# HGRN heads of a hybrid backbone layer: the attention inside a chunk on column strips of the array, block by block

## Chip, core and metric

The kernel runs on one core of a Trainium2 chip, as one program. The metric is its device time in microseconds (us); the median of three runs before the change is 1113.08 us. The engines are named as the profile names them: PE is the matrix engine, PEld its weight loads, DVE the vector engine, ACT the scalar engine, POOL the GpSimd engine, SP the engine that issues most DMAs. [...]

## What is computed

One layer of a backbone over 512 latent tokens and 256 context tokens, 1024 wide: an adaptive norm, one combined input projection, two token mixers side by side, up-projections with gates, an output projection, and a SwiGLU block. Mixer A is a gated delta rule with four heads; mixer B is HGRN2 with four heads of 128 keys and 128 values, run in both directions. The change is in mixer B:

```
def hgrn2_chunk_scan(q, k, v, log_f, s0, with_output):
    lg = jnp.cumsum(log_f, axis=3)                        # within a chunk
    ...
    pair = jnp.exp(jnp.where(incl[:, :, None], lg_c[:, :, :, None, :] - lg_c[:, :, None, :, :], -jnp.inf))
    att = jnp.einsum('bhik,bhjk,bhijk->bhij', q_c, k_c, pair)
    o = jnp.einsum('bhck,bhkv->bhcv', q_c * jnp.exp(lg_c), s) + jnp.einsum('bhij,bhjv->bhiv', att, v_c)
```

The decay between two tokens differs for each of the 128 key channels, so `att` is no plain product of two matrices.

## The kernel before

**Levels.** The kernel takes chunks of 128 tokens, so a head has four chunks `c` of latents. For each of them it builds `AT`, the transposed 128 x 128 attention of both directions in one. The diagonal comes first (called level 7), then seven levels with b = 1, 2, 4, ..., 64 (levels 0 to 6). At level b, two tokens belong together when they lie in the two halves of one block of 2b tokens; for such a pair the decay can be split at the middle of the block, so that one factor goes with the key and one with the query. `kq[:, 0, :]` holds the keys and `kq[:, 1, :]` the queries with these factors, all 512 tokens wide. The function `att(kq, lvl)` then multiplies for each chunk all 128 keys by all 128 queries into a bank `pA` of PSUM, in fp32, with four matmuls of 128 x 128 x 128 (L477). Of that product a level needs only the pairs of its blocks. A predicated copy on DVE with a mask of 0 and 1 (`lev`, 128 columns for each of the seven levels) lays them into `AT` (L482); level 7 is laid in first, whole, by a copy on ACT (L480). Between two levels, DVE and ACT move the running sums K and L to the next b and build the next `kq` (L500 to L505): two exponentials on ACT, and on DVE one product and two updates of 128 x 512.

**After the levels** come the projection of the values (`values`, L105 and L448), the transposed keys (`pk`, `pkb`, L535), the states (`pS`, L540 and L543; `h_S` on DVE, L546), the output `po` (L552 to L554), which reads `AT`, and the norm of the head (L416 to L427), whose root is taken on POOL (L421).

**The order.** The four HGRN heads (streams H0 to H3), the two pairs of delta-rule heads (G0, G2) and the gate projections (`pgate`, called F where they fill in) are emitted in turns by a hand-written plan. The streams reach the engines' lists through the framework's scheduler, which orders them by priority and by its own estimate of when each instruction could start. So an instruction that the scheduler takes to be longer or shorter also moves others. In the names, `h` is an HGRN head, `p` and `g` belong to the delta rule: `p_Z` and `p_o` are steps of a triangular inverse on DVE, `p_T` its result after two transposes (L691, L692), `p_pR`, `p_pY`, `p_pX` and `p_pRb`, `p_pYb` its matmuls on tiles of 32 x 32 and 64 x 64 of the array (L724 to L753), `p_s` its scan over chunks. `mwb` are weights of the modulation that POOL loads and DVE sums up into `acc`. H0 to H3 run between about 270 and 600 us; the rest of the time after that goes to the merge, the output projection and SwiGLU, which the change doesn't touch.

## Time and profile before

| | |
|---|---|
| median of three runs | 1113.08 us (1111.55 to 1113.27) |
| span of the profiled execution, first to last instruction | 1115.9 us |
| instructions in the profile | 15740 |
| HBM read and written | 110.51 MB and 10.49 MB |
| mean granted clock of PE | 0.980 |
| attention matmuls `h_pA`, busy | 33.0 us for the seven levels (224 records) |
| masked copies into `h_AT` on DVE | 20.5 us (28 copies) |

The profiled execution has no time besides its span, which is 2.8 us above the median; differences are therefore worked out within the profile and taken from the median. A matmul in fp32 has two records in the profile, each with its weight load, so 112 matmuls are 224 records. A record's duration runs from its start to the end of its results and overlaps with the next record; what a matmul costs PE is the distance from one start to the next. In the rows of groups, the columns are line, engine, operation, output and inputs, shape and count, then busy time and mean duration, then idle time before them and who ended it. In the rows by tile, three durations are given: least, median and greatest, in ns.

### The profile page before, as it was taken

To read this page: it belongs to the slowest core of one execution; us is meant where nothing else is said; L and a number is where in the kernel's file an instruction comes from. 1 tells how busy PE (TensorE), PEld (TensorE's weight loads), DVE (VectorE), ACT (ScalarE), POOL (GpSimd) and SP (SyncE) were. 2 spreads that over 40 slices of the span, in tenths; PEclk is the share of its full clock that TensorE was granted. 3 is DMA by queue.
4 is the path that set the end of the run, shared out by engine and by line. 5 is a ranking of instruction groups with operands and counts; after the bars stand their busy time and mean duration, and the time that the engine had idled before them with its cause. 6 is when DMAs were issued, how large, how long until landed. Compare 5 with 4: busy or idle time off the path is not lost.

```text
span 1115.9 us, 15740 instructions
## 1 busy us (share of the span) xinstructions
PE 1054.0 (94%) x6007; PEld 879.1 (79%) x6007; DVE 696.8 (62%) x1365; ACT 560.1 (50%) x1062; POOL 75.8 (7%) x132
## 2 busy tenths in 40 slices
PE   4999999979999999999988999899999999999996
PEld 3787788858897887799777887787888888888785
DVE  5896877679676868866796675586343433422424
ACT  3454568747886765887764743452222222221212
POOL 0010000220001022000201000010000000000000
PEclk9998999989999999999999999999999999999999
DMA  9943322222003213200637853455333332322222
GB/s 303 283 149 109 114 76 57 58 76 57 3 20 114 76 48 86 57 2 11 194 118 227 299 153 123 129 167 159 93 93 94 94 88 80 93 94 94 92 95 94
DMA packets 142720, 122.02 MB, mean 109 GB/s; under 512 B 5534, under 2 KB 118452, under 8 KB 142644
## 3 DMA queue, kind: packets, MB, share of 16 engines
q1 hardware_dynamic: 135907, 100.20, 30.1%
q0 software_dynamic: 4640, 17.30, 4.8%
q10 hardware_dynamic: 2096, 3.50, 1.0%
q8 instruction: 47, 0.77, 0.3%
q14 instruction: 30, 0.24, 0.1%
HBM read 110.51 MB, written 10.49 MB: 108 GB/s over the span
## 4 chain that ended last, share of the span: by engine, by line
PE 57%; DVE 10%; issue 5%; ACT 3%; POOL 2%; DMA 2%; POOLq 0%; ACTq 0%; DVEq 0%
PE pf L105 19%; PE pfo L105 10%; PE pgate L105 4%; PE pup L105 4%; PE pwo L105 3%; PE h_z L105 2%; DMA mwb<-in_mod_w_dram 2%; PE h_pA L477 2%; PE h_zv L105 1%; DVE lo L97 1%; PE p_s_pk L778 1%; PE p_s_pk L787 1%; DVE p_o L683 1%; PE p_s_pk L775 1%; DVE p_Z L685 1%
## 5 line engine op out<-in xcount | busy, mean ns | idle before, releaser
L95 ACT CAST hi<-raw 128x1024 fp32r<-128x1024 f32 (+1 forms) x137 | 135.7, 991 | 307.4 <-PE pf L105 131.2
L97 DVE TENSOR_TENSOR lo<-raw,hi 128x1024 fp32r<-128x1024 f32 (+1 forms) x137 | 157.9, 1152 | 177.5 <-ACT hi L95 176.9
L105 PE MATMUL pf<-hhi,lo 128*128 128x512 f32 (+1 forms) x368 | 142.9, 389 | 2.4 <-DVE lo L97 2.4
L105 PE MATMUL pf<-hlo,hi 128*128 128x512 f32 (+1 forms) x368 | 143.0, 390 | 0.7 <-DVE hlo L1030 0.7
L105 PE MATMUL pf<-hhi,hi 128*128 128x512 f32 (+1 forms) x368 | 142.4, 390 | 0.0
L105 PEld LDWEIGHTS pf<-hhi,lo 128*128 128x128 f32 x368 | 69.8, 190 | 18.5 <-DVE lo L97 3.3
L105 PEld LDWEIGHTS pf<-hlo,hi 128*128 128x128 f32 x368 | 69.7, 190 | 16.5 <-DVE hlo L1030 1.1
L105 PEld LDWEIGHTS pf<-hhi,hi 128*128 128x128 f32 x368 | 69.7, 190 | 15.1
L105 PE MATMUL pfo<-lo,uh 128*128 128x512 f32 x176 | 69.8, 396 | 0.1
L105 PE MATMUL pfo<-hi,ul 128*128 128x512 f32 x176 | 69.5, 395 | 0.0
L105 PE MATMUL pfo<-hi,uh 128*128 128x512 f32 x176 | 68.7, 395 | 0.0
L105 PE MATMUL pgate<-hhi,lo 128*128 128x512 f32 x144 | 60.6, 422 | 6.7 <-DVE lo L97 6.7
L105 PE MATMUL pgate<-hhi,hi 128*128 128x512 f32 x144 | 61.1, 424 | 1.8 <-ACT hi L95 1.8
L105 PE MATMUL pgate<-hlo,hi 128*128 128x512 f32 x144 | 59.8, 416 | 0.0
L1053 DVE TENSOR_TENSOR sg<-sg,pf 128x512 f32<-128x512 f32 x22 | 15.1, 688 | 53.2 <-PE pf L105 53.2
L821 DVE SCALAR_TENSOR_TENSOR acc<-mwb,sc,acc 128x256 f32<-128x256 f32 x72 | 34.3, 482 | 13.0 <-DMA mwb<-in_mod_w_dram 11.7
L261 DVE SCALAR_TENSOR_TENSOR macc<-mw,sc,macc 128x256 f32<-128x256 f32 x96 | 40.0, 479 | 0.0
L105 PEld LDWEIGHTS pfo<-lo,uh 128*128 128x128 f32 x176 | 33.1, 188 | 8.7 <-DVE lo L97 1.0
L105 PEld LDWEIGHTS pgate<-hhi,lo 128*128 128x128 f32 x144 | 28.5, 198 | 14.4 <-DVE lo L97 9.2
L105 PE MATMUL h_z<-hhi,hi 128*128 128x512 f32 x96 | 39.3, 410 | 0.3 <-ACT abT L365 0.3
L105 PE MATMUL h_z<-hlo,hi 128*128 128x512 f32 x96 | 39.4, 411 | 0.0
L105 PEld LDWEIGHTS pfo<-hi,uh 128*128 128x128 f32 x176 | 32.9, 188 | 8.2 <-ACT hi L95 0.6
(422 smaller groups left out, 2566.3 us busy)
## 6 DMA issues: line engine op xcount, KB each, us to landing
raw<-in_ffn_w_in_dram SPq DMA_DIRECT2D x44, 512.0 KB, 3.9
raw<-in_w_in_dram SPq DMA_DIRECT2D x37, 512.0 KB, 3.9
raw<-in_ffn_w_out_dram SPq DMA_DIRECT2D x22, 512.0 KB, 3.5
mwb<-in_mod_w_dram POOLq DMA_DIRECT2D x18, 512.0 KB, 4.9
mw<-in_mod_w_dram SPq DMA_DIRECT2D x16, 512.0 KB, 6.3
mwe<-in_mod_w_dram POOLq DMA_DIRECT2D x7, 1024.0 KB, 6.2
gdram<-gt SPq DMA_DIRECT2D x24, 256.0 KB, 2.4
raw<-in_w_in_dram SPq DMA_DIRECT2D x18, 256.0 KB, 3.0
```

The costliest lines, as they stand in the source:

```text
L95: nc.scalar.copy(hi[:, :, :], raw[:, :, :])
L97: nc.vector.tensor_tensor(lo[:, :, :], raw[:, :, :], hi.bitcast(F32), op=ALU.subtract)
L105: nc.tensor.matmul(ps, a[u](k), b[v](k), start=(start and n == 0), stop=(stop and n == tot - 1))
L261: nc.vector.scalar_tensor_tensor(acc[:, :], mws[d][:, k, :], col, acc[:, :], op0=ALU.mult, op1=ALU.add)
L477: nc.tensor.matmul(pA[:, P * c:P * c + P], kq[:, 0, P * c:P * c + P], kq[:, 1, P * c:P * c + P], start=True, stop=True)
L683: nc.vector.tensor_tensor(ov, Z[:, r + 1:32, r:r + 1].to_broadcast([P, 31 - r, r]), Z[:, r:r + 1, 0:r].to_broadcast([P, 31 - r, r]), op=AL ...
L685: nc.vector.tensor_tensor(Z[:, r + 1:32, 0:r], Z[:, r + 1:32, 0:r], ov, op=ALU.add)
L775: nc.tensor.matmul(pk[:, 0:P], KTt[:, g, :], S[t][:, :], start=True, stop=True)
L778: nc.tensor.matmul(pk[:, P:2 * P], N[:, d, e, g, :], rt[:, :], start=True, stop=True)
L787: nc.tensor.matmul(pk[:, 2 * P:3 * P], kend[:, :], u[:, :], start=True, stop=True)
L821: nc.vector.scalar_tensor_tensor(acc[:, :], mw[:, k - k0, :], sc[:, k:k + 1], acc[:, :], op0=ALU.mult, op1=ALU.add)
L1053: nc.vector.tensor_tensor(sg[:, :], sg[:, :], pgu[1][:, :], op=ALU.mult)
```

## The change

The product of a level is computed only where the level keeps something. For the levels 0 to 4 and the diagonal (level 7), everything kept lies in the 32 x 32 blocks on the diagonal: a matmul takes 32 keys as weights on a strip of 32 columns of the array (all 128 rows, the key channels) and 32 queries, so each chunk has four matmuls, one on each strip. They write a new small tile `AD` (128 x 4 x 32) through a mask of 32 columns. Level 5 multiplies each block of 32 keys by its neighbour's queries, and level 6 each block of 64 keys by the other 64 queries, on strips of 64 columns. Nothing of levels 5 and 6 needs a mask: they are copied into `AT` by ACT, one copy for each strip (4 and 2). After level 4, POOL copies the four blocks of `AD` into `AT`. The mask's load shrinks from 896 to 160 columns.

```
-    lev = [(r // (2 * b) == c // (2 * b)) & (r // b != c // b) for b in LEVELS]
+    r, c = r % NB, c[:, 0:NB]
+    lev = [(r // (2 * b) == c // (2 * b)) & (r // b != c // b) for b in LEVELS[0:NSM]]
...
             AT = hg.tile([P, 4, P], F32, name=n + "AT", tag="AT")
+            AD = hg.tile([P, 4, NB], F32, name=n + "AD", tag="AD")
             def att(kq, lvl):
+                w = 64 if lvl == 6 else NB
                 pA = bank("ha", f"{n}pA{lvl}")
                 for c in range(4):
-                    nc.tensor.matmul(pA[:, P * c:P * c + P], kq[:, 0, P * c:P * c + P], kq[:, 1, P * c:P * c + P],
-                                     start=True, stop=True)
+                    for j in range(P // w):
+                        kt0, qt0 = P * c + w * j, P * c + w * (j ^ (lvl in (5, 6)))
+                        nc.tensor.matmul(pA[w * j:w * j + w, w * c:w * c + w], kq[:, 0, kt0:kt0 + w], kq[:, 1, qt0:qt0 + w],
+                                         start=True, stop=True, tile_position=(0, w * j))
+                pAv = pA[:, 0:4 * w].rearrange("p (c i) -> p c i", i=w)
                 if lvl == 7:
-                    nc.scalar.copy(AT[:, :, :], pA.rearrange("p (c i) -> p c i", i=P))
+                    nc.scalar.copy(AD[:, :, :], pAv)
+                elif lvl < NSM:
+                    nc.vector.copy_predicated(AD[:, :, :], lev[:, NB * lvl:NB * lvl + NB].unsqueeze(1).to_broadcast([P, 4, NB]), pAv)
                 else:
-                    nc.vector.copy_predicated(AT[:, :, :], lev[:, P * lvl:P * lvl + P].unsqueeze(1).to_broadcast([P, 4, P]),
-                                              pA.rearrange("p (c i) -> p c i", i=P))
+                    for j in range(P // w):
+                        s = slice(w * j, w * j + w)
+                        nc.scalar.copy(AT[s, :, w * (j ^ 1):w * (j ^ 1) + w], pAv[s, :, :])
+                if lvl == NSM - 1:
+                    for j in range(P // NB):
+                        s = slice(NB * j, NB * j + NB)
+                        nc.gpsimd.tensor_copy(AT[s, :, s], AD[s, :, :])
```

NB is 32 and NSM is 5. A head has 32 matmuls of attention before and 120 after (7 x 16 and 8). The other lines of the diff only drop comments, so line numbers after the first lines differ: L477 becomes L486, L482 becomes L492, L691 becomes L708.

The scheduler makes another order of the rest, from H0's attention on. Counted along PE's whole list, neighbouring matmuls differ in the shape of the array that they use (128 x 128; 32 x 32; 64 x 64; 128 rows by strips of 32 or of 64) 32 times before and 86 times after.

PE at the start of H0's attention; `g3_k_zl` is a projection of the delta rule. Before:

```order
L105 MATMUL g3_k_zl_3569<-hhi_73,lo35_3564 128x512
L477 MATMUL h0_pA7_3184<-h0_kqd_3178 128x128 x4
L477 MATMUL h0_pA0_3195<-h0_kq0_3190 128x128 x4
L105 MATMUL g3_k_zl_3569<-hhi_73,hi35_3562 128x512
L105 MATMUL g3_k_zl_3569<-hlo_74,hi35_3562 128x512
```

The same place now:

```order
L108 MATMUL g3_k_zl_3666<-hhi_73,lo35_3661 128x512
L486 MATMUL h0_pA7_3185<-h0_kqd_3179 32x32 x16
L486 MATMUL h0_pA0_3208<-h0_kq0_3203 32x32 x16
L108 MATMUL g3_k_zl_3666<-hhi_73,hi35_3659 128x512
L108 MATMUL g3_k_zl_3666<-hlo_74,hi35_3659 128x512
L108 MATMUL g3_k_zl_3666<-hhi_73,lo35_3661 128x512
L486 MATMUL h0_pA1_3233<-h0_kq1_3228 32x32 x16
L108 MATMUL g3_k_zl_3666<-hhi_73,hi35_3659 128x512
L108 MATMUL pgate2_2455<-hhi_73,lo20_2460 128x512
```

Sixteen matmuls on strips stand where four whole ones stood, level 1 (`pA1`) comes earlier among the projections, and a gate (`pgate2`) is drawn between them.

DVE at the end of the second triangular inverse (`p2_Z`, `p2_o`), with the first levels of H3 around it. Before:

```order
L685 TENSOR_TENSOR p2_Z_4221<-p2_Z_4221,p2_o29_4348 128x2x29
L502 TENSOR_TENSOR h3_kq1_5151<-h3_q_4949,h3_E1_5152 128x512
L683 TENSOR_TENSOR p2_o30_4351<-p2_Z_4221 128x30
L685 TENSOR_TENSOR p2_Z_4221<-p2_Z_4221,p2_o30_4351 128x30
L482 COPY_PREDICATED h3_AT_5125<-lev_864,h3_pA0_5143 128x512
L691 STREAM_TRANSPOSE p2_T1_4355<-p2_Z_4221 128x32x32
L692 STREAM_TRANSPOSE p2_T2_4356<-p2_Z_4221 128x32x32
L482 COPY_PREDICATED h3_AT_5125<-lev_864,h3_pA1_5156 128x512
```

The same place now:

```order
L519 TENSOR_TENSOR h3_kq4_5445<-h3_q_5143,h3_E4_5446 128x512
L702 TENSOR_TENSOR p2_Z_4415<-p2_Z_4415,p2_o29_4542 128x2x29
L522 TENSOR_TENSOR h3_L_5142<-h3_L_5142 128x2x16x16
L700 TENSOR_TENSOR p2_o30_4545<-p2_Z_4415 128x30
L492 COPY_PREDICATED h3_AD_5320<-lev_864,h3_pA4_5450 128x128
L702 TENSOR_TENSOR p2_Z_4415<-p2_Z_4415,p2_o30_4545 128x30
L521 TENSOR_TENSOR h3_K_5141<-h3_K_5141,h3_L_5142 128x2x8x32
L708 STREAM_TRANSPOSE p2_T1_4549<-p2_Z_4415 128x32x32
L709 STREAM_TRANSPOSE p2_T2_4550<-p2_Z_4415 128x32x32
```

Before, the transposes stood behind H3's level 0; now they stand behind its level 4, among the steps of the inverse.

POOL around H2's attention; `mwb` are loads of modulation weights, `h2_ss` belongs to the norm of the head. Before:

```order
L819 DMA mwb400_5534<-in_mod_w_dram 128x4x256
L819 DMA mwb404_5540<-in_mod_w_dram 128x4x256
L819 DMA mwb410_5548<-in_mod_w_dram 128x4x256
L819 DMA mwb414_5554<-in_mod_w_dram 128x4x256
L819 DMA mwb420_5596<-in_mod_w_dram 128x4x256
L819 DMA mwb424_5602<-in_mod_w_dram 128x4x256
L819 DMA mwb430_5610<-in_mod_w_dram 128x4x256
L421 TENSOR_TENSOR h2_ss_6140<-h2_ss_6140,mhalf_102 128x4
```

The same place now:

```order
L836 DMA mwb400_5825<-in_mod_w_dram 128x4x256
L836 DMA mwb404_5831<-in_mod_w_dram 128x4x256
L500 COPY h2_AT_6190<-h2_AD_6191 32x4x32 x4
L836 DMA mwb410_5839<-in_mod_w_dram 128x4x256
L836 DMA mwb414_5845<-in_mod_w_dram 128x4x256
L836 DMA mwb420_5887<-in_mod_w_dram 128x4x256
L836 DMA mwb424_5893<-in_mod_w_dram 128x4x256
L424 TENSOR_TENSOR h2_ss_6528<-h2_ss_6528,mhalf_102 128x4
```

The four copies stand in the middle of the weight loads, and the root of the norm one load earlier.

More of the change, by code (lines that the diff above doesn't have):

```diff
@@ L26 @@
 LEVELS = (1, 2, 4, 8, 16, 32, 64)
+NB = 32
+NSM = 5
 PADN = 8 * 68 + 260
@@ L331, in body @@
             columns(1)
[L332 to L333 removed]
+            lev = cp.tile([P, NSM * NB], U8, name="lev")
+            levf = s1.tile([P, NSM * NB], F32, name="levf")
             nc.sync.dma_start(levf[:, :], T["lev"])
```

2 lines of the change are left out of this document (removed).

## The prediction

> **What bounds the kernel now.** The page first: the busy share of each engine, then the slices.
>
> ```profile
> PE 1054.0 (94%) x6007; PEld 879.1 (79%) x6007; DVE 696.8 (62%) x1365; ACT 560.1 (50%) x1062; POOL 75.8 (7%) x132
> PE   4999999979999999999988999899999999999996
> ```
>
> PE is busy nearly everywhere, so a change pays where it shortens PE's own list or removes a wait of PE. Because a share is an average, the second view is the table by stretch over the 330 us in which the HGRN heads run.
>
> ```profile
> core 0: us, PE busy (x) PEld busy (x) DVE busy (x) ACT busy (x) POOL busy (x), PEclk, DMA share, GB/s
> 270.00:300.00 30.00, 28.43 (x433) 25.06 (x432) 22.93 (x42) 25.32 (x59) 0.90 (x2) 1.00 0.14 37
> 300.00:340.00 40.00, 40.00 (x322) 36.88 (x320) 30.20 (x73) 34.91 (x101) 1.01 (x1) 1.00 0.07 21
> ...
> 450.00:500.00 50.00, 48.23 (x561) 42.34 (x560) 36.62 (x70) 40.66 (x91) 0.91 (x2) 0.97 0.12 33
> ...
> 540.00:600.00 60.00, 52.99 (x309) 45.54 (x308) 50.32 (x99) 36.64 (x70) 9.03 (x12) 0.97 0.51 155
> sum 330.00, PE 312.54 PEld 273.33 DVE 250.31 ACT 237.29 POOL 36.98; mean PE 39.07 PEld 34.17 DVE 31.29 ACT 29.66 POOL 4.62
> ```
>
> PE idles 330.0 - 312.5 = 17.5 us of it. DVE is near its limit only in the last stretch, ACT in the second. The third view is what PE waits for there.
>
> ```profile
> PE pgate L105 <- DVE lo L97: 3.1, 3, 1.5
> PE h__pt L426 <- ACT h_on L423: 3.0, 3, 2.1
> PE p_pR L724 <- DVE p_T L692: 2.9, 2, 1.5
> PE p_pt L426 <- ACT p_on L423: 2.2, 3, 1.1
> PE h_pv L448 <- ACT h_Zv L444: 2.0, 1, 2.0
> PE h_pS L540 <- DVE h_S L546: 0.8, 1, 0.8
> ...
> PE h_pkb L535 <- DVE h_AT L482: 0.6, 1, 0.6
> PE h_pA L477 <- DVE h_kq L502: 0.4, 1, 0.4
> ```
>
> Nearly nothing is waited for in the attention itself. DVE accounts for 3.1 + 2.9 + 0.8 + 0.6 + 0.4 = 7.8 us of PE's waits; the rest is latency of norms and of copies on ACT. So the first term is PE's own work, the second the part of 7.8 us that a lighter DVE gives back.
>
> **Term 1, the attention on PE.** What it costs now:
>
> ```profile
> 277.51 1.05 PE L477 MATMUL h_pA<-h_kqd 128*128 128x128 f32 x8
> 278.40 1.06 PE L477 MATMUL h_pA<-h_kq 128*128 128x128 f32 x8
> ```
>
> Eight records (four matmuls) take 278.40 - 277.51 = 0.89 us from start to start, 0.111 us each. There are 4 heads x 8 products = 32 such groups: 28.5 us.
>
> A product on strips of 32 columns has 16 matmuls, 32 records. No row has strips with all 128 rows. The nearest are tiles of 32 x 32:
>
> ```profile
> 282.43 1.40 PE L724 MATMUL p_pR<-p_T,p_N 32*32 32x32 f32 x48 [1.37 <-DVE p_T L692]
> ...
> 476.14 0.21 PE L730 MATMUL p_pY<-p_T 32*32 32x32 f32 x1
> 476.14 0.21 PE L733 MATMUL p_pX<-p_T 32*32 32x32 f32 x1
> ...
> 476.41 0.19 PE L730 MATMUL p_pY<-p_T 32*32 32x32 f32 x1
> 476.42 0.19 PE L733 MATMUL p_pX<-p_T 32*32 32x32 f32 x1
> ```
>
> In the first row 48 records, mostly six matmuls after each other on one tile, take (1.40 - 0.19) / 47 = 26 ns each, and up to 32 ns where neighbours start one behind the other on one tile (an estimate from their half-width: 0.111 us / 4 = 28 ns of streaming, and some ns for the start). In the other rows `p_pY` and `p_pX` alternate between two tiles with the same rows of the array and different columns; 18 records start within 0.28 us, 16 ns each. Two tiles therefore run at the same time. The change alternates among four strips, so its pace lies between 8 ns (all four at once, a quarter of 32) and 32 ns (one after the other). I take 16 ns, the pace of the row that is nearest in kind: 32 x 16 = 0.51 us a product, and 28 x 0.51 = 14.3 us; the ends are 7.2 and 28.7 us. Level 6 has 8 matmuls on two strips of 64, 16 records of half the 0.111 us: 0.45 us with both strips at once and 0.9 us without, so 1.8 us for four heads (end 3.6).
>
> [...]
>
> Changing the shape of the array costs time too:
>
> ```profile
> 486.54 0.49 PE L477 MATMUL h_pA<-h_kq 128*128 128x128 f32 x2
> 486.96 0.91 PE L753 MATMUL p_pYb<-p_N,p_T 64*64 64x64 f32 x12
> 487.80 0.60 PE L477 MATMUL h_pA<-h_kq 128*128 128x128 f32 x3
> ```
>
> From 486.54 to 487.80, two records of 128 columns (0.22 us) and twelve of 64 (12 x 0.056 = 0.67 us) take 1.26 us. So a change out and back costs 1.26 - 0.89 = 0.37 us; I take 0.35. The order has 86 such changes where it had 32, so 54 / 2 = 27 more round trips: 9.5 us. Where PE had to wait anyway they cost less, so 7 us is the lower end. Sum of term 1: 14.3 + 1.8 + 9.5 - 28.5 = **-2.9 us**. With four strips at once 7.2 + 1.8 + 9.5 - 28.5 = -10.0, serially 28.7 + 3.6 + 9.5 - 28.5 = +13.3.
>
> **Term 2, DVE.**
>
> ```profile
> L482 DVE COPY_PREDICATED h_AT<-lev,h_pA x28: 699/734/752, 282.2 to 584.3; 128x512 f32<-128x512 uint8 x28
> L546 DVE SCALAR_TENSOR_TENSOR h_S<-h_S,h_ed,h_pS x24: 336/344/349, 313.9 to 591.7; 128x128 f32<-128x128 f32 x24
> ```
>
> Eight masked copies fall away (levels 5 and 6): 8 x 0.734 = 5.9 us. Twenty shrink from 512 to 128 columns. No masked copy of 128 columns is shown; the nearest operation of that size that reads PSUM takes 0.344 us, so each saves 0.39 us, 7.8 us together. DVE sheds 13.7 of 250 us. Most of it frees DVE while PE has gates and projections to do, which hide it. What PE gains is bounded by 0 and the 7.8 us of waits on DVE. I take **-1.5 us**: the `p_T` and the `lo` waits shorten by a copy or two each. It is nearer to zero because the freed DVE is 5% of its load, and because the order puts H3's levels 1 to 4 ahead of the second inverse's transposes, which gives back part of what the copies save there.
>
> **Term 3, ACT and POOL.**
>
> ```profile
> L480 ACT COPY h_AT<-h_pA x4: 567/586/588, 278.6 to 565.7; 128x512 f32<-128x512 f32 x4
> L538 ACT COPY h_kt<-h_pkb x8: 257/266/299, 312.1 to 588.4; 128x128 f32<-128x128 f32 x8
> L756 ACT COPY p_N<-p_pYb x8: 462/474/475, 297.5 to 491.6; 64x384 f32<-64x384 f32 x8
> L663 POOL TENSOR_TENSOR p_E<-p_E,sq x16: 726/742/1548, 201.9 to 424.7; 128x256 f32<-128x256 f32 x16
> L582 POOL MEMSET g_k_pad<- x4: 103/116/132, 99.0 to 263.7; 128x16 f32 x4
> ```
>
> ACT gets 16 copies of 32 x 128 for level 5 (0.27 us each, the row with as many columns, 4.3 us) and 8 of 64 x 256 for level 6 (between 0.27 and 0.47 us, say 0.37, 3.0 us); the diagonal's four shrink from 0.586 to 0.27 us (-1.3 us). That is 6.0 us more of 237 us. These copies wait on PE, and behind them on ACT stand the scan's copies and the next exponentials. PE has projections and gates to cover them, so I take **+0.5 us**; the ends are 0 and, if nothing covers them, 6.0.
>
> POOL gets four copies a head, each between 0.116 and 0.742 us by the nearest rows: 0.5 to 3.0 us. Their reader is `po`, which comes after levels 5 and 6, the transposes and the states, so they cost nothing while that cover lasts; for H2, where they stand behind a load that waits for its buffer and in front of four more, the cover may go. I take 0, and as the far end 3.0 us once. The shorter mask load saves nothing that PE waits for (it lies far ahead of H0).
>
> **The sum** is -2.9 - 1.5 + 0.5 = -3.9 us within the profiled span of 1115.9 us. From the median of 1113.08 us that gives **1109.2 us**.
>
> **Rivals.** (1) *All four strips run at once.* The alternating rows speak for it, since two tiles already do and three kinds of tile are seen nearly together. Against it is that 128 rows on each strip read four times the data at once. It gives -10.0 - 1.5 + 0.5 = -11.0, 1102 us. (2) *The strips run one after the other*, on the far side: the place is the 28 groups, the price 32 ns a record, and it decides from about 19 ns on, where 896 records x 19 ns = 17.2 us uses up what the products save (28.5 - 1.8 - 9.5). With +13.3 - 1.5 + 0.5 = +12.3 it gives 1125 us. [...] For it is only that no row shows strips with all rows; against it are the rows at 16 ns. (3) *The new order takes the gain back*: H3's first five levels now precede the transposes on DVE. Four levels more in front of them, with three operations of some 0.6 us and a copy of 0.3 us each, are 8 us of DVE work before `p_pR` may start; PE has the projection `h2_z` and a gate moved there as cover, and the wait that was 1.5 us could become 6 to 8 us. That gives some +3 us, 1116 us. (4) *It doesn't matter*: PE sheds work, but ACT's latencies, not PE, set the stretch at 300 to 340 (34.9 of 40 us busy); 1112 to 1114 us.
>
> **How the numbers follow.** Chances: forecast (pairs, 1106 to 1112) 0.42; (1) 0.23; (2) 0.10; (3) 0.13; (4) 0.12. The likeliest gives 1109.2 us. For 8 times in 10 the range leaves out most of (2) and the lowest edge of (1): 1101 to 1120 us. About 0.2% (2.2 us) is what a measurement of this kernel can tell from no change. Faster by more than that: (1) and most of the forecast, 0.60. Slower: (2), and most of (3), 0.21. Within: 0.19.
>
> **What would show it.** In the changed profile, the start-to-start time of a product on strips: 0.5 us plus the change of shape if term 1 is right, about 0.3 us for rival 1, 1.0 us for rival 2. PE's busy time between 270 and 600 us should fall by a few us. The masked copies should take near 0.34 us each. The wait of `p_pR` for `p_T` at H3 tells rival 3: 1 to 3 us is the forecast, 6 us and more the rival. A wait of `po` for a copy on POOL would break term 3. The forecast is wrong if a change of shape to strips costs much more than 0.35 us, or if PE's granted clock (1.00 and 0.97 in the rows above) falls in these stretches.

## The result and the profile after

The changed kernel takes **1139.76 us** (median of 4 runs, 1137.64 to 1142.19), the kernel before, measured beside it, 1112.32 us (4 runs, 1111.55 to 1113.27). The ratio is 1.0254, with a 95% interval of 1.0233 to 1.0274: slower by some 27 us, far outside the range of the prediction. The profiled execution of the changed kernel took 1139.19 us, with a span of 1137.4 us. That is 21.5 us more than the span before, which was itself above its median; the trace therefore shows most of the loss, not all.

The page first, the busy shares and the slices of the granted clock:

```profile
PE 1063.9 (94%) x6711; PEld 875.9 (77%) x6711; DVE 683.0 (60%) x1357; ACT 566.3 (50%) x1086; POOL 85.6 (8%) x148
PEclk9998999989999999968999989999999999999999
```

DVE lost 13.8 us of work and ACT gained 6.2, as meant. PE has less to compute and is yet busy 9.9 us longer; a 6 and an 8 stand in the clock's row, about 480 to 540 us. Before, that place read 9 throughout. The table by stretch (columns as in the prediction) says which stretches lost:

```profile
340.00:370.00 30.00, 24.61 (x154) 19.93 (x152) 19.61 (x45) 19.86 (x51) 6.90 (x7) 0.94 0.39 123
370.00:410.00 40.00, 35.53 (x393) 29.44 (x392) 31.21 (x58) 29.82 (x59) 5.74 (x9) 0.96 0.20 54
...
450.00:500.00 50.00, 42.38 (x593) 35.77 (x593) 39.93 (x85) 37.06 (x70) 2.53 (x6) 0.88 0.15 42
500.00:540.00 40.00, 39.97 (x329) 36.31 (x327) 15.43 (x40) 25.02 (x76) 0.19 (x1) 0.73 0.01 1
...
sum 330.00, PE 305.04 PEld 258.01 DVE 223.00 ACT 237.16 POOL 41.42; mean PE 38.13 PEld 32.25 DVE 27.88 ACT 29.64 POOL 5.18
```

In the same 330 us PE is busy 305.0 us where it was 312.5. The prediction named this fall as a sign that its first term holds. Read alone it misleads: PE is less busy because it waits more, and the granted clock is 0.88 and 0.73 where it was 0.97 and 1.00.

Stretches cut at fixed times hold different work in the two kernels. The fair stretch runs from 270 us to the first product of `pf`, the feed-forward block, which all kernels reach with the same work done; the rest of the span takes 392.9 us here and 394.5 before. Before:

```profile
270.00:721.43 451.43, 431.44 (x3043) 369.31 (x3041) 323.81 (x650) 296.90 (x658) 38.42 (x50) 0.99 0.34 104
```

After:

```profile
270.00:744.52 474.52, 441.19 (x3747) 365.96 (x3747) 310.70 (x642) 304.40 (x683) 48.37 (x66) 0.95 0.32 99
```

The stretch grew by 23.1 us. PE's idle time (length less busy) grew from 20.0 to 33.3 us. The records of the clock hold only 1.00 and 0.50; the time at 0.50 grew from 10.2 to 51.9 us, and PE is busy for 10.2 and 47.6 us of it. Projections of 512 columns start 0.43 us apart in a window at half clock (before, 471.78 us on) and 0.23 at full clock. If all PE work at half clock takes twice as long, 23.8 - 5.1 = 18.7 us of busy time come from that, and PE's work at full clock fell by 8.9 us (from 431.4 - 5.1 = 426.3 to 441.2 - 23.8 = 417.4). So: **work -8.9, waits +13.3, clock up to +18.7**. The last is an estimate and an upper end: the measured factor is below two (0.43 / 0.23), and a part of that work stands beside waits on copies, as in the 32 x 32 part of the second inverse, which at half clock lasted 11.4 us where it had lasted 12.0.

Where the idle time lies is shown by the same stretch in three parts: up to the first `p_pR` of the second triangular inverse, the inverse (to its last `p_pYb`), and behind it. Before:

```profile
270.00:469.70 199.70, 190.71 (x1479) 165.79 (x1478) 155.83 (x336) 146.24 (x344) 21.94 (x31) 1.00 0.22 62
469.70:491.40 21.70, 21.70 (x389) 19.07 (x389) 10.97 (x17) 18.09 (x46) 0.74 (x1) 0.92 0.01 2
491.40:721.43 230.03, 219.04 (x1180) 184.44 (x1178) 157.01 (x298) 132.57 (x269) 15.75 (x18) 0.99 0.47 149
```

After:

```profile
270.00:489.79 219.79, 202.77 (x2057) 170.34 (x2057) 157.94 (x349) 156.10 (x367) 30.15 (x43) 0.98 0.20 57
489.79:517.10 27.31, 24.04 (x402) 22.08 (x403) 5.63 (x9) 19.62 (x52) 0.74 (x1) 0.53 0.01 2
517.10:744.52 227.42, 214.38 (x1291) 173.54 (x1290) 147.13 (x285) 128.68 (x265) 17.47 (x22) 0.97 0.47 150
```

PE idles 9.0 us in the first part before and 17.0 after, 0 and 3.3 us in the inverse, 11.0 and 13.0 us behind it. So most of the new waits lie ahead of the second inverse, and the inverse itself, with most of the half clock, lasts 5.6 us longer. (The first part grows by 20.1 us also because PE now does more of `h2_z` in it.)

PE's waits in that stretch, longest first (engine, line waited for, releaser, us in total, times, longest):

```profile
PE p_pt L429 <- ACT p_on L426: 6.6, 3, 3.2
PE p_pR L741 <- DVE p_T L709: 3.5, 2, 2.2
PE p_pY L747 <- ACT p_T L744: 3.3, 2, 2.8
PE h_pA L486 <- DVE h_kq L519: 3.2, 3, 2.7
...
PE h_pA L486 <- ACT h_kqd L507: 2.1, 1, 2.1
```

`h_pA` waited 0.4 us on `h_kq` and 0.2 on `h_kqd` before, `p_pt` 2.2 us, and `p_pY` for nothing. So three kinds of waits grew: those of the attention, whose operands now come later than PE has finished the level before and the work around it; those of the inverse next to it; and, by the most (4.4 us), that of `p_pt`, where a pair of delta-rule heads ends and PE waits for the norm on ACT. No run isolates the last.

The second triangular inverse shows how waits become a slow clock. PE's timeline of the changed kernel at its start (start, duration, operation, idle time before it):

```profile
487.36 0.28 PE L108 MATMUL h_z<-chi,lo 128*128 128x256 f32 x1
489.79 1.40 PE L741 MATMUL p_pR<-p_T,p_N 32*32 32x32 f32 x48 [2.16 <-DVE p_T L709]
491.12 0.63 PE L486 MATMUL h_pA<-h_kq 128*32 128x32 f32 x32
494.50 0.25 PE L747 MATMUL p_pY<-p_T 32*32 32x32 f32 x1 [2.75 <-ACT p_T L744]
```

The projections `h2_z` are over, and two waits of 2.16 and 2.75 us follow each other with little between. The windows of 3.4 us in which the granted clock changes, from there on (the number before DMA share and GB/s is the clock):

```profile
487.80:491.20 3.40, 1.41 (x56) 1.37 (x60) 3.40 (x6) 2.94 (x6) 0.74 (x1) 1.00 0.00 0
491.20:494.60 3.40, 0.65 (x36) 0.51 (x38) 0.59 (x1) 3.32 (x9) 0.00 (x0) 0.50 0.02 5
494.60:498.00 3.40, 3.40 (x114) 3.40 (x115) 0.00 (x0) 3.04 (x11) 0.00 (x0) 0.50 0.02 5
...
515.10:518.50 3.40, 3.40 (x23) 3.06 (x22) 0.00 (x0) 1.21 (x3) 0.00 (x0) 0.50 0.00 0
518.50:521.90 3.40, 3.40 (x17) 3.28 (x17) 1.39 (x4) 2.74 (x10) 0.00 (x0) 0.50 0.01 2
521.90:525.30 3.40, 3.40 (x30) 3.26 (x28) 2.25 (x5) 2.41 (x8) 0.00 (x0) 1.00 0.03 7
```

A window with 1.41 us of work is followed by half clock, and the clock stays low for nine windows, 30.7 us, though PE is busy 3.40 of 3.40 us in most of them. The same place before:

```profile
467.40:470.80 3.40, 1.86 (x47) 1.39 (x46) 3.37 (x5) 2.67 (x6) 0.74 (x1) 0.98 0.00 0
470.80:474.20 3.40, 3.40 (x16) 2.73 (x15) 0.69 (x1) 3.34 (x8) 0.00 (x0) 0.52 0.00 0
474.20:477.60 3.40, 3.40 (x92) 2.78 (x92) 1.55 (x3) 2.32 (x7) 0.00 (x0) 1.00 0.00 0
```

The clock fell there too, for one window. But `h2_z` and H3's full products stood behind `p_pR`; 16 records fill the window at half clock, and the next is at 1.00.

### The profile page after: what moved, and what is told of

Same layout as the page of the kernel before. It is cut to its first block, busy times and chain, and to the rows that moved or that the text cites. A ratio compares the mean times of both kernels' runs of the same rounds, so it can differ in the third digit from the quotient of the medians.

```text
span 1137.4 us, 17202 instructions
## 1 busy us (share of the span) xinstructions
PE 1063.9 (94%) x6711; PEld 875.9 (77%) x6711; DVE 683.0 (60%) x1357; ACT 566.3 (50%) x1086; POOL 85.6 (8%) x148
## 4 chain that ended last, share of the span: by engine, by line
PE 41%; issue 5%; DVE 4%; DMA 4%; ACT 2%; POOL 1%; POOLq 0%; SPq 0%; ACTq 0%
PE pf L108 18%; PE pfo L108 10%; PE pwo L108 3%; PE pup L108 3%; DMA mwb<-in_mod_w_dram 2%; DVE lo L100 1%; DMA mwe<-in_mod_w_dram 1%; PE pgate L108 1%; PE p_s_pk L795 1%; ACT hi L98 1%; PE p_s_pk L804 1%; PE p_pYb L770 1%; DMA raw<-in_w_up_a_dram 0%; PE p_s_pk L792 0%; DVE acc L838 0%
## 5 line engine op out<-in xcount | busy, mean ns | idle before, releaser
L108 PE MATMUL h_z<-hhi,lo 128*128 128x512 f32 x96 | 39.0, 406 | 0.0
```

The lines of the kernel that those rows point to most:

```text
L108: nc.tensor.matmul(ps, a[u](k), b[v](k), start=(start and n == 0), stop=(stop and n == tot - 1))
```

## The experiments

Main theory: the strips are cheaper on PE, but the order that the scheduler made with them leaves PE without full-array work beside the short chains of the HGRN heads and of the inverse; what is saved comes back as waits, and the windows with little work cost the clock. Rivals: A, the strips themselves are slow (their changes of shape); B, the POOL copies, or the load on ACT, are the new wait. For the first group PE's order was written out as a chain of order edges, so that work and order can be exchanged; the other engines are scheduled anew around it.

**Strips in the order of before** (all strips code kept; the list `ORDER` is PE's order before):

```
+        chain, at = [], {}
+        for item in ORDER.split():
+            n, c = item.split("*")
+            c = int(c) * (len(made[n]) // 4 if "pA" in n else 1)
+            a = at.get(n, 0)
+            chain += made[n][a:a + c]
+            at[n] = a + c
+        for e, l in zip(chain, chain[1:]):
+            tc.add_manual_dep(l, e.name, ...)
```

> The changed kernel (strips, small masks, all its copies) with the order of TensorE's instructions of the kernel before, written out as a chain from the first product to the end of the output projection: where the kernel before had one of the four products of a level, its four (level 6: two) strips stand. Nothing else is set; the other engines' orders follow from it. Theory 1 (the loss is the new order, through the clock and the waits; the strips themselves save 20 us of PE less 10 to 14 us of shape changes): half-clock windows between 270 and 745 us add up to at most 14 us, and the time is 1098 to 1115 us, that is 25 to 40 us below the changed kernel. Rival A (the strips, the changes of the array's shape and the copies cost it wherever they stand): 1130 to 1142 us. In between, 1116 to 1129 us: part of the loss is in the strips.

It took 1134.96 us (1133.15 to 1139.13), ratio 1.0206 [1.0167, 1.0245]. Missed: the old order alone does not save the strips. Its stretch to `pf`:

```profile
270.00:742.08 472.08, 438.29 (x3741) 363.82 (x3739) 310.67 (x640) 302.12 (x680) 46.67 (x66) 0.95 0.32 99
```

It idles 33.8 us, with 47.8 us at half clock, as the changed kernel does.

**Full products in the new order** (before's kernel with the same chain of edges; the list is the changed kernel's order, and a group of strips there counts as the product it belongs to):

> The kernel before (full 128x128 products, full masks, no strips) with the order of TensorE's instructions of the changed kernel, written out as a chain in the same way: a full product stands where the first of its strips stood. No operation is added or removed. Theory 1: without any strip the time rises to 1125 to 1145 us, with 20 us or more at half clock between 270 and 745 us, most of it in and behind the second inverse. Rivals A and B: no strips and no new copies, 1110 to 1117 us.

It took 1145.1 us (1145.02 to 1145.54), ratio 1.029 [1.0264, 1.0315]: at the upper edge of what was expected. 37.6 us of its stretch are idle and 41.7 us at half clock, without a single strip; 13.7 us of the half clock lie in the second inverse, against 30.7 in the changed kernel. So each half of the change costs 22 to 32 us when put alone into the kernel before, and both together cost 27; the costs do not add. In the new order the strips with their copies even gain some 6 us (ratio 1.029 against the 1.0236 of the control below). This is what one would see if an order fits the durations for which it was made. Rival A falls as the main cause, and so does the idea that the order alone is to blame.

**The copies of POOL moved to ACT**, PE's order held:

```
-                        nc.gpsimd.tensor_copy(AT[s, :, s], AD[s, :, :])
+                        nc.scalar.copy(AT[s, :, s], AD[s, :, :])
```

> The changed kernel with the four copies of the diagonal blocks of each head moved from GpSimd (654 ns each in the mean, and 35.8 us of waiting on that engine) to ScalarE, and TensorE's order held as the changed kernel has it. Theory 1: these copies cover nothing that PE waits for (0.3 us), so the time stays within 4 us of the changed kernel, 1136 to 1144 us. Rival B (the copies on GpSimd, or what queues behind them there, are the cost): 1120 to 1133 us.

1143.08 us (1139.94 to 1147.33), ratio 1.0273 [1.0238, 1.0309]: no gain. Rival B falls for POOL; the load on ACT was not tested.

**Control: the changed kernel with its own order written out.**

> The control: the changed kernel with TensorE's order written out as the chain that the scheduler gave it, and nothing else. The instructions stand on every engine as in the changed kernel. All theories: 1137 to 1143 us, as the changed kernel; otherwise the runs with written-out orders can't be compared with it.

1137.96 us (1133.87 to 1142.74), ratio 1.0236 [1.0201, 1.0272]: the written-out chain itself costs nothing that can be measured.

**Work added to keep the clock.** Unused 128 x 128 products were put into the waits of the second inverse. The first form left the order to the scheduler, which then moved `h2_z` too:

```
+            def warm(cnt):
+                ps = bank("fa", f"{n}warm{cnt}") if h0 and cnt else None
+                for i in range(cnt if h0 else 0):
+                    nc.tensor.matmul(ps[:, 0:128], Zf[:, P * (i % 8):P * (i % 8) + P], ident, start=True, stop=True)
+            warm(20)
...
+                warm(24 * (e == 0))
```

> The changed kernel with work added and none taken away: 44 full-array 128x128 fp32 products whose result nobody reads, 20 ahead of the second inverse's first tiles and 24 between its first and second group, where PE idled 2.15 and 2.75 us. They cost 4.9 us of PE at full clock (0.11 us apart) and 9.4 us at half. Theory 1: PE stays full where it idled, the clock holds or comes back within one or two windows of 3.41 us, and the time falls by 8 to 16 us, to 1124 to 1132 us, although work was added. Rivals A and B: nothing that costs time is removed, so the time rises by 0 to 5 us, 1139 to 1145 us.

1134.29 us (1128.77 to 1139.32), ratio 1.0206 [1.0166, 1.0245]: lower than the changed kernel although work was added, short of the expected size. The expectation took half of the true cost: an fp32 product is two records, 0.22 us, so 44 are 9.9 us. Its profiled execution, the slowest of the four (1139.32 us), has 3.4 us at half clock in the second inverse and a stretch of 474.4 us, as long as the changed kernel's. Two forms with PE's order held followed: the same 20 and 24 products, and then 9, 11 and 12 in three waits.

> The changed kernel, its own order of TensorE's instructions written out as a chain and so held, with the 44 full-array products of the second experiment set into it at two places: 20 ahead of the second inverse's first tiles, 24 between those and the next group, where PE waited 2.15 and 2.75 us. Unlike in the second experiment, no projection changes its place. The added products cost 4.9 us of PE at full clock, most of it in time in which PE stood still. Theory 2 (the granted clock, decided in windows of 3.41 us by how much of the array is in use, is the largest part of the loss): the half-clock stretch of 30.7 us there shrinks to 10.3 us or less, and the time falls by 7 to 14 us to 1126 to 1133 us, with nothing taken away. If the clock is a by-product (the stretch is bound by ScalarE, and PE only waits for it): the stretch shrinks as well, but the time stays, 1138 to 1145 us.

> As the run before with TensorE's order of the changed kernel held and unused full-array products set into the second inverse, but sized to the waits: a 128x128 fp32 product is two records of 0.112 us, so that the 20 and 24 of the run before took 4.62 and 5.62 us, twice what the waits of 2.15 and 2.75 us have room for, and PE fell idle for 2.81 us in a third place (ahead of the third group of tiles), where the clock then fell. Now 9, 11 and 12 products stand in the three places (2.0, 2.5 and 2.7 us, 7.1 us in all, nearly all of it in time in which PE stands still). Theory 2: at most 6.8 us at half clock in the second inverse instead of 30.7 us, and a time 8 to 14 us below the changed kernel with its order held, 1126 to 1132 us. If the clock is a by-product of a stretch that ScalarE bounds: within 3 us of the changed kernel with its order held.

They took 1144.28 us (1142.91 to 1144.91) and 1143.77 us (1140.71 to 1146.47): missed. In the first the added groups are twice as long as the waits; this is PE's timeline in that kernel:

```profile
490.99 4.62 PE L94 MATMUL p_warm<-sq,p_Z 128*128 128x128 f32 x40
497.26 5.62 PE L94 MATMUL p_warm<-sq,p_Z 128*128 128x128 f32 x48
```

The second had the right length, but both read `p_Z`, whose buffer the inverse uses again, and ACT's copies into it (from 489.86 us in the control) could start only 9.6 us later, here in the second form's timeline of ACT:

```profile
499.46 2.06 ACT L734 COPY p_X<-p_T 32x384 f32<-32x384 f32 x4
```

So these two tell little of the clock. The last form reads constants alone, holds PE's order and ACT's order through the inverse, and adds 37 products (9, 11, 7 and 10; 8.2 us):

```
+                    nc.tensor.matmul(ps[:, 0:128], sq[:, P:2 * P], sq[:, 2 * P:3 * P], start=True, stop=True)
```

> The changed kernel with TensorE's order held as before and ScalarE's order through the second inverse held too, and 37 unused full-array products at the four places of the second inverse where TensorE waits: 9, 11, 7 and 10 (2.0, 2.5, 1.6 and 2.2 us). They read constants only. In the two runs before, the products read the tile of the triangular solve and so kept its buffer, which a later tile of the inverse reuses; ScalarE's copies into that tile then ran 8 us later (499.5 us against 489.9 us in the control), and TensorE waited 3.28 us for them and lost the clock there. With that gone nothing but the products differs from the control. Theory 2, with its place (in the 32x32 part of the inverse ScalarE is the bound, so half clock costs nothing there; behind it, from 503 to 522 us, TensorE is): no half clock in the inverse beyond 6.8 us, and a time 6 to 10 us below the control (1138.0 us), 1128 to 1132 us. If the clock is a by-product throughout: within 3 us of the control, 1135 to 1141 us.

1133.47 us (1132.1 to 1136.14), ratio 1.0182 [1.0153, 1.0211]. With 8.2 us of work added and nothing taken away it lies 4.5 us below the control; by the ratios, which stand against runs of the kernel before on two chips, -0.54% with an interval of about 0.46% either way (the two half-widths, 0.36% and 0.29%, added in squares). The direction is as expected, the size smaller than the 6 us at least that were expected, and the interval only just leaves out zero. The control's windows at this place:

```profile
489.40:492.80 3.40, 1.23 (x65) 1.07 (x62) 1.45 (x3) 3.35 (x8) 0.24 (x1) 0.68 0.03 5
492.80:496.20 3.40, 2.65 (x91) 2.65 (x92) 0.00 (x0) 3.02 (x11) 0.00 (x0) 0.50 0.00 0
...
506.40:509.80 3.40, 3.40 (x33) 3.04 (x31) 1.22 (x1) 1.05 (x4) 0.00 (x0) 0.50 0.00 0
```

and with the added products:

```profile
489.40:492.80 3.40, 3.40 (x70) 3.17 (x65) 1.02 (x3) 3.33 (x9) 0.00 (x0) 1.00 0.02 5
492.80:496.20 3.40, 3.12 (x125) 3.04 (x125) 0.00 (x0) 3.22 (x12) 0.00 (x0) 1.00 0.02 5
...
506.40:509.80 3.40, 3.40 (x54) 2.98 (x53) 0.90 (x1) 2.89 (x7) 0.00 (x0) 1.00 0.00 0
```

Half clock in the inverse falls from 30.7 to 6.8 us. From the first `p_pRb` to the last `p_pYb` the inverse takes 9.1 us where the control takes 15.9, and from the first `p_pR` to there, the part with most of the added products, 15.9 us where it took 11.4. So the slow clock costs time by itself; how much of its duration, this run cannot say, since a part of the added work costs time too.

**Padding.** The strips in the old order, plus four unused full-array products of 64 columns at every level, first in all heads, then in two (here H0 and H3):

```
+                for c in range(4 * (h in (0, 3))):
+                    nc.tensor.matmul(pA[:, 256 + 64 * c:320 + 64 * c], kq[:, 0, P * c:P * c + P], kq[:, 1, P * c:P * c + 64],
+                                     start=True, stop=True)
```

> The strips in the old order of TensorE's instructions (as in the run above) with work added and none taken away: behind the strips of every level of every head four full-array products of 64 columns, written to columns that nobody reads (8 records of about 0.058 us, 0.46 us a level, 14.7 us in all at full clock). With them a level costs PE about 1.08 us (0.27 of strips, 0.35 of shape changes, 0.46) against 0.89 us in the kernel before. Theory 2, formed after the run above (the stages are not bound by PE; work taken from PE there does not shorten them but thins the windows of 3.41 us in which the clock is decided, and at half clock the rest costs more than the strips save): the half-clock time between 270 and 745 us falls from 47.7 to at most 25 us and the time falls by 8 to 25 us, to 1110 to 1127 us, although PE has more to do than in the kernel before. Rival A (strips, shape changes and copies cost the time by themselves): the added work comes on top, 1138 to 1150 us.

> As the run with the padding in all heads, but the padding stands only in H0 and H3, whose levels lie beside the two inverses; H1 and H2 have their bare strips. Theory 2, with its place (the clock is lost where levels and quadrant tiles lie together): most of the gain of the padding is here, 1110 to 1126 us, and at or below the run with the padding in all heads. Rival A: 7.4 us of work on top of 1135 us, 1136 to 1144 us.

> The other half: padding in H1 and H2 only, bare strips in H0 and H3. Theory 2 with its place: the half-clock stretches at the two inverses stay, 1130 to 1142 us. If padding helps here as much as in H0 and H3, the place is wrong and any thinning of PE's work costs clock. Rival A: 1136 to 1144 us.

All heads: 1139.8 us (1135.36 to 1150.2). H0 and H3: 1133.61 us (1129.86 to 1140.32). H1 and H2: 1144.16 us (1138.43 to 1145.69). All three missed. The first lies in the range that was given for rival A (1138 to 1150), the second between the two ranges, the third above both; there the half clock at the two inverses stayed as expected (6.8 and 20.5 us). One reason is that a record with 64 moving columns takes 0.11 us, as one with 128 does (0.111 us in the kernel before): the padding is 0.89 us a level, 28.6 us over all heads, twice what was expected. The balance below shows 29.6 us more work for these 256 records. With it on top of 1135 us, rival A would give some 1164 us for the first. What the padding does shows in this row of the kernel with all heads padded, against the strips in the old order above:

```profile
270.00:748.10 478.10, 454.52 (x3991) 382.99 (x3990) 312.01 (x638) 303.20 (x679) 46.10 (x66) 0.98 0.32 98
```

28.6 us of work on PE lengthen the stretch by 6.0 us and the median by 4.8. Idle time falls from 33.8 to 23.6, half clock from 47.8 to 20.5, and none is left at the second inverse. In H0 and H3, beside the two inverses, 14.3 us of work cost nothing that can be measured (1133.6 against 1135.0); in H1 and H2 they cost 9.2. That is not because PE had 14.3 us to spare in H0 and H3: idle time falls by 6.0 us over the stretch, and the rest is paid for by the clock (47.8 to 23.9 us at half).

**Other plans.** `PLAN` is the list from which the order starts. Moves of the gate and projection items, with the strips (changed kernel's `PLAN` first):

```
-  ... H0:99 F:3 G2:4 H1:99 G2:4 F:1 G2:99 N:1 H3:99 aT:1 H2:1 X H2:99
+  ... H0:99 G2:4 F:3 H1:99 G2:4 F:1 G2:99 N:1 H3:99 aT:1 H2:1 X H2:99
```

> The changed kernel with one item of the plan moved: the three gate projections of F:3 are emitted behind the next four steps of the second delta pair instead of ahead of them. In the order that this gives, 34 records of H2's first projection and of pgate8 stand between the tiles of the second inverse (7.0 us of full-array work up to the third scan step; the changed kernel has none there, the kernel before 6.6 us). Strips, small masks and copies are as in the changed kernel. Theory 1 (the loss is the new order: the inverse lost its cover, PE idled, its granted clock fell to half for 30.7 us, and quadrant tiles did not bring it back): the half-clock stretch at the inverse shrinks to at most 7 us, the time falls by 15 to 25 us against the changed kernel, to 1113 to 1125 us or less. Rival A (the strips themselves, or the changes of the array's shape, keep the clock down or cost the time wherever they stand): 1135 to 1142 us. Rival B (the copies on ScalarE and GpSimd are the cost): 1135 to 1142 us as well.

1123.36 us (1115.88 to 1125.32), ratio 1.0096 [1.0058, 1.0134]. Moving one item takes away 16 us, more than half of the loss. The time was met, the reason that was given for it was not: the half clock at the second inverse should have shrunk to at most 7 us, and the trace has 23.9 us there. In the stretch to `pf` the kernel idles 8.5 us less than the changed kernel, and halving gives 4.7 us for the clock (38.2 us of busy time at half clock instead of 47.6). Here the waits were the larger part. With a second move:

```
-  ... H1:99 G2:4 F:1 G2:99 ...
+  ... H1:99 G2:8 F:1 G2:99 ...
```

> The changed kernel, its order left to the scheduler, with two moves in the plan: the gates of F:3 behind the next four steps of the second delta pair (as in the first experiment), and H1's remaining steps followed by eight instead of four steps of that pair before the last gate. 8.2 us of projections stand between the tiles of the second inverse (7.0 us in the first experiment, 6.6 us in the kernel before). Theory 2: like the first experiment or a little better, 1112 to 1125 us. Rival A: 1135 to 1142 us.

1119.22 us (1114.4 to 1119.63), ratio 1.0047 [1.0026, 1.0068]: met, and the best time with strips. Its stretch:

```profile
270.00:725.99 455.99, 433.84 (x3762) 358.61 (x3761) 315.91 (x648) 305.21 (x685) 44.26 (x66) 0.98 0.34 103
```

Idle 22.2 us, half clock 20.5. Three plans more moved other items: `H2:1` ahead of `H3:99` alone, the same with the two moves, and a third move beside the two.

```
-  ... N:1 H3:99 aT:1 H2:1 X H2:99
+  ... N:1 H2:1 H3:99 aT:1 X H2:99
...
-  ... F:1 G0:99 H0:99 ...
+  ... G0:99 F:1 H0:99 ...
```

> The changed kernel with another single item of the plan moved: H2's first step ahead of H3's remaining steps instead of behind them, which puts H2's second projection and pgate8 between the tiles of the second inverse (9.1 us of full-array work there). Theory 1: as for the run with the gates moved, at most 7 us at half clock there and 1105 to 1122 us. Rivals A and B: 1135 to 1142 us.

> The changed kernel with the two moves of the plan of the run before that was left to the scheduler (1119.2 us) and a third: H2's first step ahead of H3's remaining steps. H3's levels then stand behind the second inverse and 11.9 us of projections between its tiles. Theory 2: at most 10 us at half clock from 450 to 560 us, and 1108 to 1120 us; it beats the kernel before (below 1110 us) only if the waits too fall to what they are there. If the clock is a by-product: 1117 to 1125 us.

> The same two moves, and one gate projection of the first pair's end emitted behind that pair's last steps. 8.7 us of projections stand between the tiles of the second inverse, spread more evenly. Theory 2: 1110 to 1121 us. If the clock is a by-product: 1117 to 1125 us.

They took 1131.23, 1121.6 and 1120.7 us. The first is the counterpart of the plan with one move: the half clock at the second inverse is 6.8 us as was expected, and the time is 9 us above the expected range, with 35.8 us idle. The second lies just above its range, the third met it; both also lie in the range for a clock that is a by-product (1117 to 1125), so they don't decide. The last has the least half clock of all strips kernels (17.1 us) and idles 28.6 us:

```profile
270.00:726.17 456.17, 427.60 (x3736) 352.81 (x3735) 310.32 (x638) 301.66 (x679) 45.45 (x66) 0.98 0.34 102
```

One more run asked whether the earlier `h2_z` is the cause by itself: before's kernel with a higher priority for that item.

```
+                pull = 1000 * (item == "H2:1")
+                tc.cur_priority -= pull
                 filler(int(n)) if name == "F" else run(name, int(n))
+                tc.cur_priority += pull
```

> The kernel before, without strips, with one priority changed: the first step of H2 (its first projection) is pulled ahead of what is ready beside it, so that its records stand ahead of the second inverse instead of between its tiles (9.6 us of tiles in a row without a projection; 1.2 us at most in the kernel before up to the second group). No operation is added or removed. Theory 1: the full-width kernel now loses its clock at the inverse too: two or more further windows at half clock there, and the time is 5 to 20 us above the kernel before (1118 to 1133 us). Rival A (strips) and rival B (copies): there are no strips and no new copies, so within 3 us of the kernel before (1110 to 1116 us).

1114.3 us (1110.97 to 1122.57, 10 runs), ratio 1.0039 [1.0017, 1.0062]: missed; only 6.8 us of the inverse are at half clock. The early `h2_z` does little by itself; that H3's full products still stand among the inverse's tiles may be why.

The balance of the stretch to `pf` for the kernels that carry the argument, in us (work is busy time less half of PE's busy time at half clock; added is unused work within it):

| kernel | length | idle | half clock | of it at the second inverse | work | added |
|---|---|---|---|---|---|---|
| before | 451.4 | 20.0 | 10.2 | 3.4 | 426.3 | 0 |
| after | 474.5 | 33.3 | 51.9 | 30.7 | 417.4 | 0 |
| strips, old order | 472.1 | 33.8 | 47.8 | 27.3 | 416.1 | 0 |
| full products, new order | 482.9 | 37.6 | 41.7 | 13.7 | 427.0 | 0 |
| strips, old order, padded | 478.1 | 23.6 | 20.5 | 0 | 445.7 | 28.6 |
| control | 473.8 | 33.5 | 51.8 | 30.7 | 416.4 | 0 |
| control with 37 products | 469.4 | 28.6 | 28.0 | 6.8 | 427.5 | 8.2 |
| strips, one move in the plan | 461.2 | 24.8 | 41.0 | 23.9 | 417.3 | 0 |
| strips, `H2:1` ahead of `H3:99` | 471.1 | 35.8 | 31.3 | 6.8 | 420.0 | 0 |
| strips, two moves | 456.0 | 22.2 | 20.5 | 3.4 | 423.6 | 0 |
| strips, three moves | 456.2 | 28.6 | 17.1 | 3.4 | 419.1 | 0 |

The length does not follow the half clock at the second inverse: 23.9 us there go with 461.2, 6.8 us with 471.1. The plans also move some work across the 270 us mark, so their rows are good to a few us.

**The clock between runs of one kernel.** Every run's span and mean granted clock are on record, and with only 1.00 and 0.50 granted they give its time at half clock: 2 x (1 - mean clock) x span. The runs of one kernel have the same instructions and differ in it; the plan with one move, for one, has a span of 1114.1 us at 0.976 and of 1123.4 at 0.968. Over all 79 runs of the kernels other than before, each against the mean of its own kernel, 1 us more at half clock goes with 0.34 us more time (standard error 0.02, correlation 0.88). By this rate the 41.7 us more at half clock in the changed kernel would be some 14 us, an estimate. It is an association, since the waits may change along with the clock.

## Why the prediction was wrong

**The cause of the sum's failure.** The prediction costed each term on the order and the clock of before. It had written that the new order costs nothing but rival 3's wait, and had put the clock's fall only among the things that would make it wrong, at no price and no chance. These are the two terms that came: waits +13.3 us and half clock up to +18.7 us in the trace, against 8.9 us of work saved. That the order on the engines is at issue, the moved plan items show, since they change nothing else and the best takes back 20 us; the exchange of order and work shows that neither the strips nor the new order is the cause alone. That the clock costs time by itself, the 37 products show. The share of each within the loss is not settled: the two do not simply go together (the plan with one move against `H2:1` moved alone), and a changed order moved both.

**Term 1 (-2.9 predicted).** The direction was right and the size was off in the change's favour. A product on four strips between two projections:

```profile
478.45 0.40 PE L108 MATMUL h_z<-hhi,lo 128*128 128x512 f32 x1
478.78 0.46 PE L486 MATMUL h_pA<-h_kq 128*32 128x32 f32 x32
479.17 0.50 PE L108 MATMUL h_z<-hhi,hi 128*128 128x512 f32 x1
```

From 478.45 to 479.17 are 0.72 us; less the 0.23 us between projections, 0.48 us (before rounding, 0.716 - 0.232) are the product and the change of shape out and back. The 32 records start within about 0.27 us (0.46 less the 0.19 us that one lasts), 8 ns each: all four strips run at once, rival 1's end. The change of shape is then about 0.21 us, not 0.35, which came from a group split by tiles of 64 x 64. Level 6 takes 0.71 us, worked out in the same way in H2. Undisturbed, the term would be 28 x 0.48 + 4 x 0.71 - 28.5 = -12.2 us, and the work of the balance above fell by 8.9 (by 10.2 in the strips in the old order). The strips share all 128 rows, and 8 ns is a quarter of the 32 ns estimated for one strip after the other.

**Rival 1** therefore had the right mechanism and gave 1102 us, of all the farthest from the measured time: it held PE's work to be the bound. The step that failed stands in the first paragraph of the prediction: PE is busy nearly everywhere, so a change pays where it shortens PE's list. It left out that the next operands must be there when PE's list gets shorter. The likely reading is that full products had filled time in which the chain of exponentials, `kq` products and copies was not ready, so that two limits lay close together where the profile of before showed hardly a wait. This is argued, not shown; the balance fits it, since in the plan with three moves 7.2 us less work than before come back as 8.6 us more idle time. The longest wait of the attention shows another limit, the order on DVE. In H1 `h_pA` waits 2.7 us for `h_kq` (rows of the timelines of ACT, DVE and PE):

```profile
377.15 0.63 ACT L517 ACTIVATE h_E<-h_L 128x512 f32<-128x512 f32 x1 [0.67 <-DVE h_L L522]
377.72 1.22 DVE L100 TENSOR_TENSOR lo<-raw,hi 128x1024 fp32r<-128x1024 f32 x1
379.75 0.68 DVE L519 TENSOR_TENSOR h_kq<-h_q,h_E 128x512 f32<-128x512 f32 x1
380.58 0.46 PE L486 MATMUL h_pA<-h_kq 128*32 128x32 f32 x32 [2.67 <-DVE h_kq L519]
```

ACT has `h_E` ready at 377.78, but DVE first works through the `lo` of a weight and a step of the delta rule (378.86, 0.78 us) and comes to `h_kq` 2 us later. So a part of these waits hangs on DVE's list, which the scheduler had reordered as well.

**Rival 3** named the right place with the wrong price. The `p_pR` wait went from 1.54 to 2.16 us in the second inverse, which the prediction counted for its forecast (1 to 3 us). It had not asked what stands behind the wait: the cover `h2_z` now lay ahead of it, so the next wait, `p_pY` for ACT's copies, was bare as well; behind a window with 1.41 us of work the clock was at half, and in the next, with 0.65 us, PE had as little to do. The 32 x 32 part of the inverse (first `p_pR` to first `p_pRb`) lasts 12.0 us before and 11.4 after, so half clock shows no cost there. What pays is the 64 x 64 part, 9.8 us before and 15.9 after, where the median record of `p_pYb` lasts 288 ns over both inverses where it was 218:

```profile
L770 PE MATMUL p_pYb<-p_N,p_T x96: 217/288/366, 297.2 to 517.1; 64*64 64x64 f32 x96
```

**Term 2** was right in what DVE sheds (13.8 us; 13.7 predicted) and wrong in what PE gains from it, -1.5 us: PE's waits on DVE rose from 7.8 to 11.4 us. **Term 3** was right in its work, 6.2 us (6.0) on ACT. POOL's copies are dear and harmless, as the views by tile show (least, median, greatest ns; then who waited):

```profile
L492 DVE COPY_PREDICATED h_AD<-lev,h_pA x20: 290/299/310, 279.2 to 593.9; 128x128 f32<-128x128 uint8 x20
L500 POOL COPY h_AT<-h_AD x16: 279/654/1624, 306.3 to 596.4; 32x128 f32<-32x128 f32 x16
...
  POOL h_AT L500: 35.8, 4
```

POOL waits 35.8 us for `AD`, but `po` never waits for POOL, and the copies on ACT gave no gain. Rival 2 (serial strips) and rival 4 (no effect) are out.

**Open.** No version with strips beat the kernel before. With much of the clock regained (20.5 and 17.1 us at half clock, 10.2 before) the best two still idle 22 and 29 us where it was 20. Whether an order made by hand for the strips would give the 9 to 12 us was not shown; strips in some heads only, and the level 5 and 6 copies on another engine than ACT, were not tried.

## What to carry to other kernels

A kernel that shows PE at 94% with hardly a wait can still be balanced on a chain of other engines, the likely reading here; ask of every stage how much PE time could go before the next wait appears, and price only that much. When work is taken from PE beside a short serial chain, name what full-array work covers the chain's waits afterwards, and write down what the clock would do without it (here 30.7 us at half in the second inverse). A scheduler that is given new durations makes a new order; a run of the old order with the new work, and one of the reverse, show whether order or work is to blame, or, as here, that neither is alone. And when an experiment meets its time, look whether its trace shows the reason too: the plan with one move did not.

## What the runs showed of the hardware

**In these traces the clock fell mostly behind windows in which PE had little to do, and came back behind windows that used most of the array.** Between 270 us and `pf`, the granted clock in the traces of before and after holds each value for a whole number of windows of 3.41 us (from 1 to 64). In the window 494.60 to 498.00 above PE is busy for all 3.40 us and stays at 0.50; its records are tiles of 32 x 32. It returned only after 518.50 to 521.90, which is full of 128 x 128 records. But in the kernel with 37 products, in which the window of 506.40 to 509.80 holds tiles of 64 x 64 as the control's does, full clock is kept. Two numbers were worked out for each window of 3.41 us between 270 us and `pf` in the 19 traces (2,595): the busy share of PE, and the share of the array at work. The second is the time of the records at full clock, from start to start (0.231, 0.120 and 0.112 us for 512, 256 and at most 128 columns on the whole array; 58 and 25 ns for tiles of 64 x 64 and 32 x 32; 31 and 8 ns for strips of 64 and 32 columns), weighted by the tile's part of the array and doubled at half clock. At full clock, of the windows in which PE was busy for less than 0.4, all 54 were followed by half clock; from 0.4 to 0.6, 25 of 66; from 0.99 on, 1 of 1,758, although 105 of these had less than half of the array at work. In between it fell too, as in the kernel with 37 products behind 492.80 to 496.20, where PE was busy for 3.12 of 3.40 us. At half clock, of the windows in which PE was busy for 0.99 or more, all 37 with a share of the array under 0.6 were followed by another, 11 of 15 from 0.6 to 0.8, and 4 of 90 from 0.8 on. This fits the traces; only the run with 37 products tested it.

In the changed kernel the window with the wait of 2.16 us (from 487.80 us on, PE busy for 1.41 of 3.40 us) was followed by half clock; the wait of 2.75 us stands in the next window, which was at half clock already.

**Four strips of 32 columns with all 128 rows** overlapped in the changed kernel: 8 ns from one record to the next, where one lasts 0.19 us (478.78 us). **A 128 x 128 weight tile with 64 moving columns** was as dear in the padded kernel as with 128, 0.11 us a record. **The spread differs between kernels and sets of runs:** the kernel before stays within 1.7 us over 4 runs beside the changed kernel and within 8.3 us over 8 later ones, the plan with one move spans 9.4 us in 4 runs and before's kernel with the pulled item 11.6 us in 10, each with one and the same list of instructions. By the association of time and clock above (0.34 us for 1 us at half clock, correlation 0.88) a good part of it may be the clock; it was not shown.
